# A second weight tile fetched from ScalarE's queue, and a branch that takes its row tiles in another order

## The chip, the cores and the metric

The kernel runs on one core of one Trainium2 chip. The metric is the device time of one execution in microseconds (us). The engines are named as the profile names them: PE is TensorE (PEld its weight loads), DVE is VectorE, ACT is ScalarE, POOL is GpSimd, and SP is SyncE, which here only issues DMAs. A DMA is issued by an engine's instruction stream (SPq, ACTq and POOLq in the profile) and carried out by 16 DMA engines that all queues of the core share.

## The reference

One layer of a decoder with two token mixers side by side, 256 tokens, 2048 channels, all in float32:

```python
h = rmsnorm(x, pre_norm_g[l])
proj = h @ w_in[l]                      # 2048 x 18448
(a_q, a_k, a_v, a_g, a_lr, b_q, b_k, b_v, b_g, m_a, m_b) = jnp.split(proj, offsets, axis=-1)
gk = log_sigmoid(a_lr @ gla_gk_w2[l] + gla_gk_b[l]) / 16
o_a = rmsnorm(gla_chunked(a_q, a_k, a_v, gk), gla_norm_g[l]) * silu(a_g)
y_a = o_a @ w_branch_a[l]               # 2048 x 2048
o_b = rmsnorm(diff_attention(b_q, b_k, b_v, lam), diff_norm_g[l]) * (1 - lam_init) * silu(b_g)
y_b = o_b @ w_branch_b[l]
merged = sigmoid(m_a) * y_a + sigmoid(m_b) * y_b
x = x + rmsnorm(merged @ w_out[l], post_norm_g[l])
```

Each `@` sums over 2048 rows of a weight matrix. The order in which these rows are summed is free.

## The kernel before, in words

**Tiles.** The 2048 rows of every matrix product are cut into 16 row tiles of 128 (`KT`; a row tile's index is `kt`). The host lays the weights out in pieces, in the order in which the kernel takes them. A piece is fetched by DMA into a tile `raw`, and is then split in two: ACT copies it rounded into `hi` (L345), DVE subtracts to get the rest `lo` (L346). PE multiplies `hi` with both halves of the other operand and `lo` with its first half (L519). The other operand is split in the same way: x into the tiles `xs`, two row tiles in each.

**The start.** The first weight chunk, `v0`, comes in 16 units of 416 KB (128 x 832), one row tile each. For a unit PE does four matmuls with `hi` into banks `mm`, four with `hi` into `bg`, and two and two with `lo`. Unit 0's weight `raw_first` is fetched as two halves of 208 KB. x comes transposed in groups of 1, 1, 2, 4, 4 and 4 row tiles (`load_x`), of 128 KB for each row tile, into `xraw`. x is multiplied by the gains `pre_norm_g` on its way to `xs` (`prep_x`: L390 on ACT or, for row tile 1, L388 on DVE gives the first half, L391 on DVE the second); the gains are an input of 8 KB, `preg_s`, fetched on ACT's queue as its first instruction. All other loads at the start are issued by SP in the order in which the code is written: x row tile 0, the two halves of `raw_first`, unit 1's weight, x row tile 1, x row tiles 2 and 3, unit 2's weight, unit 3's weight, and so on.

**Order.** The compiler's scheduler sorts the instructions of each engine from the order of the code and from when it reckons that the operands are there; `tc.keep_in_program_order` pins an instruction to its place. Weights are fetched and split `AHEAD` = 4 steps before their use; `raw` has 6 buffers.

**The second branch's first operand.** The output of the first token mixer is split into `oah` and `oal` and stored to DRAM in four pairs of 512 KB tiles. Later `fetch_a` loads the pairs 0, 1, 2, 3 back with SP (L816), `oah` and then `oal` of each. The chunks `y00` to `y03` multiply them with `w_branch_a`, eight units of two row tiles to a chunk. Which pair row tile `kt` lies in is told by `a_ops`:

```python
h, j = kt // 4, kt % 4
i = 2 * (h // 2) + j // 2               # the pair
return oah[i][:, j % 2, h % 2, :], oal[i][:, j % 2, h % 2, :]
```

So the units of `y00` use the pairs 0, 1, 0, 1, 2, 3, 2, 3. Between two units of `y00` PE does six matmuls of another product, recorded at L720 (`set`).

Of the kernel before, what the change touches and what calls it, by code (L numbers as in the profile page):

```python
# [6 lines left out]
F32 = mybir.dt.float32  # L7
# [7 lines left out]
P = 128  # L15
D = 2048
S = 256
KT = D // P
# [3 lines left out]
VG = (416, 416, 416, 416, 400)  # L22
RANK = 16
AHEAD = 4
X_GROUPS = ((0, 1), (1, 1), (2, 2), (4, 4), (8, 4), (12, 4))
X_LOADS = ((), (4,), (8,), (12,), (), (), (), ())
ROWS = {"two": 2, "tok": 4, "chan": KT}
# [130 lines left out]
def order_of(n):  # L158
    return OUT_ORDER if n == OUT else ORDERS[n not in MOVED]


def chain_of(n, name):
    if n == OUT:
        return OUT_CHAINS.get(name)
    chain = PRODUCTS[name][1]
    return chain if chain is None else (chain + n) % 2
# [3 lines left out]
def hybrid_kernel(ctx: ExitStack, tc, xt, xn, preg, postg, w, w2, gkb, glag, lamv, diffg, ident_d, causal_d, lmask_d, out):  # L170
    nc = tc.nc
    pe, act, dve, pool, sp = nc.tensor, nc.scalar, nc.vector, nc.gpsimd, nc.sync

    const = ctx.enter_context(tc.tile_pool(name="const", bufs=1))
    wpool = ctx.enter_context(tc.tile_pool(name="wpool", bufs=3))
# [7 lines left out]
    def u(shape, name, dtype=F32):  # L183
        count[0] += 1
        return big.tile(shape, dtype, tag="u", name=f"{name}_{count[0]}")
# [17 lines left out]
    def f32(ap):  # L203
        return ap.bitcast(F32)
# [17 lines left out]
    def piece(key, q):  # L222
        size = sizes[key]
        at = begins[key] + q * size * P
        return w[at : at + P * size].rearrange("(p n) -> p n", p=P)
# [4 lines left out]
    def block(n, name, unit, add=True, which=None, queue=pool):  # L230

        chain, (kh, g) = chain_of(n, name), which or PRODUCTS[name][2]
        src = piece(SETS[n][g], 2 * kh + unit // 2)[:, 1024 * (unit % 2) : 1024 * (unit % 2) + 1024]
        dst = chains[chain][unit] if chain is not None else plain[n, name, unit]
        if add:
            return pool.dma_start(dst, src, accum_op=ALU.add)  # L236
        return queue.dma_start(dst, src)  # L237
# [40 lines left out]
    def emit_half():  # L278
        j = emitted[0]
        emitted[0] += 1  # L280
        key, unit = steps[j]
        if j in begin:
            start_sets()
        if j == begin_out:
            start_out()
        if j == begin_out + 8:
            for n in range(4):
                plain[OUT, "p2", n] = u([P, 1024], "plain")
                block(OUT, "p2", n, add=False)
        if isinstance(key, int):  # L290
            i = set_steps.index((key, unit))
            name, part = order_of(key)[unit // 4], unit % 4
            if key == 1 and part == 0 and unit < 24:
                ahead = PRODUCTS[order_of(key)[unit // 4 + 1]][0]
                if ahead in parts_far:
                    fetch_square(ahead)
            chain, (kh, g) = chain_of(key, name), PRODUCTS[name][2]
            if (key, name, part) in plain:
                raw = plain.pop((key, name, part))
            elif chain is None:  # L300
                raw = wpool.tile([P, 1024], F32, tag="raw", name=f"raw_s{key}_{unit}", bufs=6)
                at = 1024 * (part % 2)
                sp.dma_start(raw, piece(SETS[key][g], 2 * kh + part // 2)[:, at : at + 1024])
            else:
                raw = chains[chain][part]
            hi_t = wpool.tile([P, 1024], F32R, tag="hi", name=f"hi_{j}")
            lo_t = wpool.tile([P, 1024], F32R, tag="lo", name=f"lo_{j}")
            act.activation(hi_t, raw, AF.Copy)  # L308
            dve.tensor_tensor(out=lo_t, in0=raw, in1=f32(hi_t), op=ALU.subtract)  # L309
            refill(i, key, name, part, raw)  # L310
            ready[j] = ((key, unit), hi_t, lo_t)
            return
        size = sizes[key]
        h = unit % 2
        src = piece(key, unit // 2)
        n = size // 2
        early = key == "v0"
        if j == 2:
            load_x(2, 2)
        if j == 0:  # L320
            raw = raw_0
        else:
            raw = wpool.tile([P, 1024], F32, tag="raw", name=f"raw_{key}_{unit}", bufs=6)
            i = sp.dma_start(raw[:, :n], src[:, n * h : n * h + n])
        if early:
            if j:
                tc.keep_in_program_order(i)
            if j == 1:
                load_x(1, 1)
            for kt in X_LOADS[j // 2] if h else ():  # L330
                load_x(kt, 4)
        if early:
            prep_x(j)
            if 6 <= j < 14:
                square_x(j - 6)
        if key == "o3" and j + 1 < len(steps):
            hi_t, lo_t = u([P, 1024], "keep", F32R), u([P, 1024], "keep", F32R)
        else:
            hi_t = wpool.tile([P, 1024], F32R, tag="hi", name=f"hi_{j}")
            lo_t = wpool.tile([P, 1024], F32R, tag="lo", name=f"lo_{j}")  # L340
        fine = 2 if j == 0 else 1
        for i in range(fine):
            a, b = n * i // fine, n * (i + 1) // fine
            r = raw[:, a:b]
            act.activation(hi_t[:, a:b], r, AF.Copy)  # L345
            dve.tensor_tensor(out=lo_t[:, a:b], in0=r, in1=f32(hi_t[:, a:b]), op=ALU.subtract)  # L346
        ready[j] = (key, hi_t, lo_t)
# [5 lines left out]
    def take(key):  # L353
# [3 lines left out]
        used[0] += 1  # L357
        while emitted[0] < min(j + 1 + AHEAD, len(steps)):
            emit_half()
# [6 lines left out]
    preg_s = const.tile([P, KT], F32, name="preg_s")  # L366
# [3 lines left out]
    def load_x(kt, n):  # L370
        tc.keep_in_program_order(sp.dma_start(xraw[kt // 4][:, kt % 4 : kt % 4 + n, :].rearrange("p a t -> p (a t)"), xt[P * S * kt : P * S * (kt + n)].rearrange("(p n) -> p n", p=P)))
# [3 lines left out]
    for c in (slice(0, VG[0]), slice(VG[0], 2 * VG[0])):  # L375
        tc.keep_in_program_order(sp.dma_start(raw_0[:, c], piece("v0", 0)[:, c]))
    act.preload_act_table_set("natural_log_exp_and_others")

    def x_ops(kt):
        return xs[kt // 2][:, kt % 2, 0, :], xs[kt // 2][:, kt % 2, 1, :]  # L380

    def prep_x(kt):
        i, j = kt // 4, kt % 4
        src = xraw[i][:, j, :]
        g = preg_s[:, kt : kt + 1]
        hi, lo = x_ops(kt)
        if kt == 1:
            dve.tensor_scalar(out=hi, in0=src, scalar1=g, scalar2=None, op0=ALU.mult)  # L388
        else:
            act.activation(hi, src, AF.Copy, scale=g)  # L390
        dve.scalar_tensor_tensor(out=lo, in0=src, scalar=g, in1=f32(hi), op0=ALU.mult, op1=ALU.subtract)  # L391
# [3 lines left out]
    def square_x(i):  # L395
        src = xraw[i // 2][:, 2 * (i % 2) : 2 * (i % 2) + 2, :].rearrange("p a t -> p (a t)")
        t = t2([P, 512], "xsq") if i else ssum
        tc.keep_in_program_order(act.activation(t, src, AF.Square))
        if i:
            dve.tensor_tensor(out=ssum, in0=ssum, in1=t, op=ALU.add)  # L400
# [280 lines left out]
    def start_sets():  # L681
        n = started[0]
        started[0] += 1
        while "squares" not in done:
            with tc.issue_after(latest[0]):
                next(operands, None)
        for c in range(2):
            chains[c][:] = [u([P, 1024], f"chain{c}") for _ in range(4)]
        for unit in range(4):
            tc.keep_in_program_order(block(n, "p1", unit, add=False))  # L690

    def start_out():
        for c in range(2):
            chains[c][:] = [u([P, 1024], f"chain{c}") for _ in range(4)]
        for unit in range(4):
            block(OUT, "p1", unit, add=False)
        for unit in range(4):
            block(OUT, "q7", unit, add=False, which=(1, 1))
        for unit in range(4):
            block(OUT, "q7", unit)  # L700

    def fetch_square(name):
        parts[name] = tuple(u([P, 8, P], "square", F32R) for _ in range(2))
        for t, src in zip(parts[name], parts_far[name]):
            tc.keep_in_program_order(pool.dma_start(f32(t), src))
# [469 lines left out]


    def a_ops(kt):
        h, j = kt // 4, kt % 4
        i = 2 * (h // 2) + j // 2
        return oah[i][:, j % 2, h % 2, :], oal[i][:, j % 2, h % 2, :]  # L1180

# [48 lines left out]
    first, both, raw = {}, {}, {}  # L1230
# [287 lines left out]
```

## Time and profile before

| | |
|---|---|
| time, median of 3 runs | 1090.03 us (1089.81 to 1090.1) |
| the profiled execution | 1090.54 us, of which its span in the trace is 1088.7 us |
| PE busy | 1078.1 us, 99% of the span |
| DVE, ACT, POOL busy | 871.1, 707.5, 219.6 us (80%, 65%, 20%) |
| granted TensorE clock | 0.997 |
| HBM | 276.71 MB read, 24.12 MB written, 276 GB/s over the span |

In a row of the timeline stand the start in us from the span's start, the duration in us, the engine, the line, the operation and what it writes and reads; in brackets, how long the engine was idle before it and what ended that. Rows of DMA issues give the time that the issue took, not the transfer; the time from an issue to its landing is in the DMA view (last column). L numbers are lines of this kernel; in the changed kernel the same lines stand 3 to 8 lines further down.

### The profile page before, as it was taken

What the parts mean: (1) busy time and instruction counts of PE and PEld (TensorE: products, weight loads), DVE (VectorE), ACT (ScalarE), POOL (GpSimd) and SP (SyncE); (2) the same over time, 40 slices, a digit from 0 to 9 for tenths busy, and PEclk for the clock granted to TensorE, in tenths of its full rate; (3) what the DMA queues carried; (4) which work ended last, traced back from release to release, by engine and by line L of the source; (5) the groups of instructions that cost most, each with busy time, mean ns of one, the idle gap of its engine ahead of it and who ended that gap; (6) DMA issues with size and microseconds to landing.
All of it is one profiled execution on the core that took longest, in us unless ns stands there. A gap on an engine that the chain in (4) does not pass through costs nothing.

```text
span 1088.7 us, 15454 instructions
## 1 busy us (share of the span) xinstructions
PE 1078.1 (99%) x5434; PEld 920.2 (85%) x5434; DVE 871.1 (80%) x1220; ACT 707.5 (65%) x1020; POOL 219.6 (20%) x319
## 2 busy tenths in 40 slices
PE   9999999999999999999999999999999999999996
PEld 8999888888888888888888888888888888888885
DVE  7787668997877889897887788776688687687994
ACT  8777466655656676776766767665666665536871
POOL 0112101110331222123113122222211222301100
PEclk9999999999999999999999999999999999999998
DMA  8899988598999988579989998999977999987874
GB/s 319 272 303 331 302 281 221 171 365 327 242 291 340 341 252 209 202 210 270 283 265 238 309 262 225 277 326 363 326 203 263 335 345 354 359 320 230 216 189 152
DMA packets 86286, 301.84 MB, mean 277 GB/s; under 512 B 10369, under 2 KB 11649, under 8 KB 86209
## 3 DMA queue, kind: packets, MB, share of 16 engines
q0 software_dynamic: 38560, 139.48, 49.2%
q1 hardware_dynamic: 46928, 160.33, 40.5%
q10 hardware_dynamic: 720, 1.06, 0.3%
q8 instruction: 42, 0.69, 0.2%
q14 instruction: 36, 0.29, 0.1%
HBM read 276.71 MB, written 24.12 MB: 276 GB/s over the span
## 4 chain that ended last, share of the span: by engine, by line
PE 96%; DMA 2%; DVE 0%; ACT 0%; POOL 0%; issue 0%; SPq 0%; DVEq 0%; POOLq 0%; ACTq 0%
PE mm L519 31%; PE set L720 31%; PE mm L540 16%; PE mm L542 8%; PE mm L501 2%; DMA oal<-oal_far 2%; PE bg L519 2%; PE bg L1039 1%; PE bg L906 1%; PE bg L501 1%; PE bg L1070 0%; DMA raw_v<-in_w_dram 0%; PE bg L1258 0%; PE bg L988 0%; PE bg L1077 0%; PE bg L1078 0%
## 5 line engine op out<-in xcount | busy, mean ns | idle before, releaser
L309 DVE TENSOR_TENSOR lo<-chain,hi 128x1024 fp32r<-128x1024 f32 x212 | 257.3, 1222 | 72.0 <-ACT hi L308 71.0
L308 ACT ACTIVATE hi<-chain 128x1024 fp32r<-128x1024 f32 x212 | 223.1, 1058 | 132.7 <-PE mm L519 45.0
L540 PE MATMUL mm<-xs,hi 128*128 128x512 f32 x768 | 199.6, 392 | 0.0
L236 POOL DMA_DIRECT2D chain<-in_w_dram x120 | 104.4, 874 | 436.5 <-DVE lo L309 288.1
L540 PEld LDWEIGHTS mm<-xs,hi 128*128 128x128 f32 x768 | 142.7, 188 | 28.1 <-ACT hi L345 0.5
L720 PE MATMUL set<-hi,square 128*128 128x512 f32 x512 | 139.6, 394 | 0.0
L519 PE MATMUL mm<-hi,xs 128*128 128x512 f32 (+2 forms) x512 | 118.9, 372 | 0.8 <-ACT hi L345 0.8
L542 PEld LDWEIGHTS mm<-xs,lo 128*128 128x128 f32 x768 | 104.5, 190 | 8.0 <-DVE lo L346 0.5
L720 PEld LDWEIGHTS set<-hi,square 128*128 128x128 f32 x512 | 93.4, 188 | 18.4 <-ACT qk L1168 0.7
L542 PE MATMUL mm<-xs,lo 128*128 128x256 f32 x768 | 107.2, 282 | 0.0
L720 PE MATMUL set<-hi,xs 128*128 128x512 f32 x384 | 104.8, 394 | 0.0
L519 PEld LDWEIGHTS mm<-hi,xs 128*128 128x128 f32 x512 | 94.7, 188 | 11.5 <-ACT hi L345 1.1
L346 DVE TENSOR_TENSOR lo<-raw_y,hi 128x1024 fp32r<-128x1024 f32 x64 | 78.3, 1223 | 31.0 <-ACT hi L345 30.8
L345 ACT ACTIVATE hi<-raw_y 128x1024 fp32r<-128x1024 f32 x64 | 67.9, 1061 | 53.9 <-PE mm L519 34.2
L720 PEld LDWEIGHTS set<-hi,xs 128*128 128x128 f32 x384 | 70.2, 188 | 13.3 <-ACT hi L308 0.3
L720 PE MATMUL set<-lo,square 128*128 128x512 f32 x256 | 79.2, 390 | 0.0
L237 POOL DMA_DIRECT2D chain<-in_w_dram x72 | 39.6, 556 | 159.4 <-DVE lo L309 128.9
L519 PE MATMUL mm<-lo,xs 128*128 128x512 f32 (+2 forms) x256 | 64.7, 369 | 0.0
L720 PE MATMUL set<-lo,xs 128*128 128x512 f32 x192 | 59.5, 391 | 0.0
L720 PEld LDWEIGHTS set<-lo,square 128*128 128x128 f32 x256 | 47.9, 188 | 10.9 <-DVE lo L309 0.5
L346 DVE TENSOR_TENSOR lo<-raw_dk,hi 128x1024 fp32r<-128x1024 f32 x32 | 39.1, 1222 | 18.6 <-ACT hi L345 18.6
L519 PEld LDWEIGHTS mm<-lo,xs 128*128 128x128 f32 x256 | 47.7, 188 | 5.5 <-DVE lo L346 0.3
(308 smaller groups left out, 1945.4 us busy)
## 6 DMA issues: line engine op xcount, KB each, us to landing
chain<-in_w_dram POOLq DMA_DIRECT2D x192, 512.0 KB, 10.3
raw_y<-in_w_dram SPq DMA_DIRECT2D x64, 512.0 KB, 8.0
raw_dq<-in_w_dram SPq DMA_DIRECT2D x32, 512.0 KB, 7.7
raw_dk<-in_w_dram SPq DMA_DIRECT2D x32, 512.0 KB, 7.6
raw_v<-in_w_dram SPq DMA_DIRECT2D x31, 416.0 KB, 5.4
raw_s<-in_w_dram SPq DMA_DIRECT2D x24, 512.0 KB, 8.0
raw_ag<-in_w_dram SPq DMA_DIRECT2D x24, 512.0 KB, 6.6
raw_k<-in_w_dram SPq DMA_DIRECT2D x16, 512.0 KB, 7.2
```

Of the source, the lines that this page charges most:

```text
L236: return pool.dma_start(dst, src, accum_op=ALU.add)
L237: return queue.dma_start(dst, src)
L308: act.activation(hi_t, raw, AF.Copy)
L309: dve.tensor_tensor(out=lo_t, in0=raw, in1=f32(hi_t), op=ALU.subtract)
L345: act.activation(hi_t[:, a:b], r, AF.Copy)
L346: dve.tensor_tensor(out=lo_t[:, a:b], in0=r, in1=f32(hi_t[:, a:b]), op=ALU.subtract)
L501: i = pe.matmul(out, lhs, rhs, start=first and n == 0, stop=last and n == len(pairs) - 1)
L519: i = pe.matmul(banks[g][b][:, :n], a[part][:, P * b : P * b + P], w[:, c : c + n], start=first, stop=last)
L540: i = pe.matmul(o, hi[:, c], x_pair(kt), start=kt == 0, stop=kt == KT - 1)
L542: i = pe.matmul(o[:, :S], lo[:, c], x_ops(kt)[0], start=False, stop=False)
L720: i = pe.matmul(bank, a[part], wt[:, 512 * j : 512 * j + 512], start=go, stop=end, skip_group_check=not first)
L906: pe.matmul(o, xk[:, P * c : P * c + P], xq.rearrange("p (b c t) -> p b c t", b=2, c=4)[:, :, c, :], start=i == 0, stop=i == 1)
```

## The change

The diff, with what lies between its parts left out:

```diff
+A_ORDER = (0, 1, 4, 5, 2, 3, 6, 7, 8, 9, 12, 13, 10, 11, 14, 15)
...
         if j == 0:
             raw = raw_0
+        elif j == 1:
+            raw = raw_1
         else:
             raw = wpool.tile([P, 1024], F32, tag="raw", name=f"raw_{key}_{unit}", bufs=6)
             i = sp.dma_start(raw[:, :n], src[:, n * h : n * h + n])
         if early:
-            if j:
+            if j > 1:
                 tc.keep_in_program_order(i)
...
     act.preload_act_table_set("natural_log_exp_and_others")
+    raw_1 = wpool.tile([P, 1024], F32, tag="raw", name="raw_second", bufs=6)
+    dve.tensor_copy(raw_1[:, :KT], preg_s)
+    tc.keep_in_program_order(act.dma_start(raw_1[:, : 2 * VG[0]], piece("v0", 0)[:, 2 * VG[0] :]))
...
     def a_ops(kt):
-        h, j = kt // 4, kt % 4
+        h, j = A_ORDER[kt] // 4, A_ORDER[kt] % 4
...
+    mats["w_branch_a"] = mats["w_branch_a"].reshape(KT, P, D)[list(A_ORDER)].reshape(D, D)
```

Unit 1's weight is no longer issued by SP but by ACT, into the tile `raw_second`. DVE first copies the gains into a corner of that tile; the DMA overwrites the copy, and so it can't be issued before the copy is done, nor the copy before the gains have landed. In SP's queue everything behind moves up by one place. The row tiles of `w_branch_a` and of its operand are permuted alike, so that the units of `y00` to `y03` use the pairs 0, 0, 1, 1, 2, 2, 3, 3.

The scheduler answers with another order at the start. On ACT, before (the tiles `hi` are numbered, `xs_72` holds the row tiles 0 and 1, `xs_73` 2 and 3; the rows begin behind the gains' DMA):

```order
L390 ACTIVATE xs_72<-xraw_81,preg_s 128x256
L345 ACTIVATE hi_177<-raw_first 128x416 x2
L345 ACTIVATE hi_188<-raw_v_1_183 128x832
L390 ACTIVATE xs_73<-xraw_81,preg_s 128x256 x2
L345 ACTIVATE hi_197<-raw_v_2_193 128x832
```

and in the changed kernel:

```order
L396 ACTIVATE xs_72<-xraw_81,preg_s 128x256
L383 DMA raw_second<-in_w_dram 128x832
L348 ACTIVATE hi_180<-raw_first 128x416 x2
L396 ACTIVATE xs_73<-xraw_81,preg_s 128x256 x2
L348 ACTIVATE hi_189<-raw_second 128x832
```

The issue of the DMA has come in behind x's row tile 0, and the split of unit 1's weight now stands behind x's row tiles 2 and 3 instead of ahead of them.

On DVE at the start, before (L388 and the L391 behind it are x's row tile 1):

```order
L391 SCALAR_TENSOR_TENSOR xs_72<-xraw_81,preg_s,xs_72 128x256
L346 TENSOR_TENSOR lo_178<-raw_first,hi_177 128x416 x2
L388 TENSOR_SCALAR xs_72<-xraw_81,preg_s 128x256
L391 SCALAR_TENSOR_TENSOR xs_72<-xraw_81,preg_s,xs_72 128x256
L346 TENSOR_TENSOR lo_189<-raw_v_1_183,hi_188 128x832
L391 SCALAR_TENSOR_TENSOR xs_73<-xraw_81,preg_s,xs_73 128x256 x2
```

and in the changed kernel:

```order
L382 COPY raw_second<-preg_s 128x16
L397 SCALAR_TENSOR_TENSOR xs_72<-xraw_81,preg_s,xs_72 128x256
L394 TENSOR_SCALAR xs_72<-xraw_81,preg_s 128x256
L397 SCALAR_TENSOR_TENSOR xs_72<-xraw_81,preg_s,xs_72 128x256
L349 TENSOR_TENSOR lo_181<-raw_first,hi_180 128x416 x2
L397 SCALAR_TENSOR_TENSOR xs_73<-xraw_81,preg_s,xs_73 128x256 x2
L349 TENSOR_TENSOR lo_190<-raw_second,hi_189 128x832
```

The copy is new; x's row tile 1 has moved ahead of unit 0's two `lo`, and the row tiles 2 and 3 ahead of unit 1's.

On PE in `y00`, one matmul of each of the first seven units, before (`oah_7032`, `_7139`, `_7260` and `_7270` are the pairs 0 to 3):

```order
L519 MATMUL mm_7274<-hi_7177,oah_7032 128x512
...
L519 MATMUL mm_7274<-hi_7229,oah_7139 128x512
...
L519 MATMUL mm_7274<-hi_7289,oah_7032 128x512
...
L519 MATMUL mm_7274<-hi_7331,oah_7139 128x512
...
L519 MATMUL mm_7274<-hi_7361,oah_7260 128x512
...
L519 MATMUL mm_7274<-hi_7390,oah_7270 128x512
...
L519 MATMUL mm_7274<-hi_7419,oah_7260 128x512
```

and in the changed kernel (`oah_7033`, `_7140`, `_7261` and `_7271` are the pairs 0 to 3):

```order
L525 MATMUL mm_7275<-hi_7178,oah_7033 128x512
...
L525 MATMUL mm_7275<-hi_7230,oah_7033 128x512
...
L525 MATMUL mm_7275<-hi_7290,oah_7140 128x512
...
L525 MATMUL mm_7275<-hi_7332,oah_7140 128x512
...
L525 MATMUL mm_7275<-hi_7362,oah_7261 128x512
...
L525 MATMUL mm_7275<-hi_7391,oah_7261 128x512
...
L525 MATMUL mm_7275<-hi_7420,oah_7271 128x512
```

Pair 3 is first used in the seventh unit instead of the sixth. Apart from these places, the order on the five engines differs only in a few neighbours that have changed places.

## The prediction

> **What bounds the kernel now.** I read the page's busy times and its chain first, then who made PE wait, then the two places where it did.
>
> ```profile
> PE 1078.1 (99%) x5434; PEld 920.2 (85%) x5434; DVE 871.1 (80%) x1220; ACT 707.5 (65%) x1020; POOL 219.6 (20%) x319
> ...
> PE 96%; DMA 2%; DVE 0%; ACT 0%; POOL 0%; issue 0%; SPq 0%; DVEq 0%; POOLq 0%; ACTq 0%
> ```
>
> PE is busy for 1078.1 of 1088.7 us, and 96% of the chain is PE. What isn't PE's own work can be gained only where PE waits. The waits of PE in the whole span (who waited for whom; total us, times, longest) are three:
>
> ```profile
> PE bg L434 <- DVE ones L431: 1.1, 1, 1.1
> PE mm L519 <- ACT hi L345: 0.8, 1, 0.8
> PE mm L519 <- DMA oal<-oal_far: 0.5, 1, 0.5
> ```
>
> The first lies ahead of the warm-up matmuls and isn't touched. The second is at unit 1's start, the third in `y00`: the change aims at these two. Since PE has no other wait, whatever it loses or gains at them goes through to the end.
>
> The start, in the timeline:
>
> ```profile
> 0.74 0.41 ACTq L373 DMA_DIRECT2D preg_s<-in_preg_dram  x1
> ...
> 2.12 0.43 SPq L324 DMA_DIRECT2D raw_v<-in_w_dram  x1
> ...
> 2.60 0.91 SPq L371 DMA_DIRECT2D xraw<-in_xt_dram  x2
> ...
> 3.06 0.51 ACT L390 ACTIVATE xs<-xraw,preg_s 128x256 fp32r<-128x256 f32 x1 [0.28 <-DMA preg_s<-in_preg_dram]
> 3.54 0.91 SPq L324 DMA_DIRECT2D raw_v<-in_w_dram  x2
> 3.60 0.48 DVE L391 SCALAR_TENSOR_TENSOR xs<-xraw,preg_s,xs 128x256 fp32r<-128x256 f32 x1 [2.59 <-ACT xs L390]
> 3.67 0.55 ACT L345 ACTIVATE hi<-raw_first 128x416 fp32r<-128x416 f32 x1
> 4.25 0.59 DVE L346 TENSOR_TENSOR lo<-raw_first,hi 128x416 fp32r<-128x416 f32 x1 [0.17 <-ACT hi L345]
> ...
> 4.40 1.01 PE L519 MATMUL mm<-hi,xs 128*128 128x416 f32 x4
> ...
> 4.80 0.55 ACT L345 ACTIVATE hi<-raw_first 128x416 fp32r<-128x416 f32 x1 [0.57 <-DMA raw_first<-in_w_dram]
> ...
> 5.40 1.02 PE L519 MATMUL bg<-hi,xs 128*128 128x416 f32 x4
> ...
> 6.64 0.54 PE L519 MATMUL bg<-lo,xs 128*128 128x416 f32 x2
> ...
> 7.02 0.90 ACT L345 ACTIVATE hi<-raw_v 128x832 fp32r<-128x832 f32 x1 [1.67 <-DMA raw_v<-in_w_dram]
> 7.36 0.35 DVE L388 TENSOR_SCALAR xs<-xraw,preg_s 128x256 fp32r<-128x256 f32 x1 [1.38 <-DMA xraw<-in_xt_dram]
> ...
> 7.75 0.48 DVE L391 SCALAR_TENSOR_TENSOR xs<-xraw,preg_s,xs 128x256 fp32r<-128x256 f32 x1
> ...
> 7.97 1.02 PE L519 MATMUL mm<-hi,xs 128*128 128x416 f32 x4 [0.79 <-ACT hi L345]
> 8.01 0.91 ACT L390 ACTIVATE xs<-xraw,preg_s 128x256 fp32r<-128x256 f32 x2
> 8.15 1.02 DVE L346 TENSOR_TENSOR lo<-raw_v,hi 128x832 fp32r<-128x832 f32 x1
> ```
>
> Unit 0 ends at 7.18 (6.64 + 0.54) and unit 1 begins at 7.97, 0.05 behind the end of its `hi`, which began as soon as its weight had landed. In the chain the piece is
>
> ```profile
> 2.12 4.88 DMA raw_v<-in_w_dram
> ```
>
> so the weight landed at 7.00. When the other early loads landed I work out from their issues above and their times to landing (DMA view, one narrow window for each):
>
> ```profile
> raw_first<-in_w_dram SPq DMA_DIRECT2D x1, 208.0 KB, 3.1
> ...
> xraw<-in_xt_dram SPq DMA_DIRECT2D x1, 128.0 KB, 4.7
> ...
> xraw<-in_xt_dram SPq DMA_DIRECT2D x1, 256.0 KB, 4.9
> ...
> raw_v<-in_w_dram SPq DMA_DIRECT2D x1, 416.0 KB, 5.5
> ...
> raw_v<-in_w_dram SPq DMA_DIRECT2D x1, 416.0 KB, 6.1
> ```
>
> `raw_first`'s second half lands at about 4.8 (the `hi` that waits for it starts at 4.80), x row tile 1 at 2.60 + 4.7 = 7.3, row tiles 2 and 3 at some 3.06 + 4.9 = 8.0, unit 2's weight at 3.54 + 5.5 = 9.0, unit 3's at some 4.0 + 6.1 = 10.1. Each lands behind the one issued before it.
>
> **Part A: unit 1's weight on ACT's queue.** It removes one of SP's issues (0.43 us), so x's row tiles 1, 2 and 3 and the weights behind them are issued that much earlier; that alone is worth nothing to PE, which waits for none of them.
>
> The new copy on DVE (128x16; nearest row L388 with 256 columns, 0.35 us, an upper end) can start when the gains are there, by 3.06, and is over before DVE's next step at 3.60: its cover is DVE's idle time of 2.59 us. ACT issues `raw_second` behind its first `xs`, at about 3.5, instead of SP at 2.12. The issue (0.41, the gains' row) holds up the ACT work queued behind it, `hi` of `raw_first`: 3.67 becomes some 4.0, and PE's first matmul 4.7 instead of 4.40. That is hidden: the `hi` of the second half can't start before 4.80 anyway, so `bg` starts at about 5.45 instead of 5.40.
>
> What costs is which bytes have to land before unit 1. Before, unit 1's weight was behind 8 + 128 + 416 KB; with its own 416 KB, 968 KB. Now x's 128 and 256 KB are ahead of it on SP's queue and in flight at the same time, and ACT does `xs` of the row tiles 2 and 3 ahead of unit 1's `hi`: 1352 KB have to land first. In the trace of before, the same 1352 KB were in at about 8.0. If `raw_second` is the last of them, its `hi` ends at 8.0 + 0.90 and unit 1 starts at 8.95, 1.0 later than 7.97. If x's row tiles 2 and 3 are the last, their `xs` (0.91) come in between: 9.85. If unit 2's weight, issued by SP at about the same time as `raw_second` by ACT, takes its share too, `raw_second` may land as late as 9.0: 9.95, or +2.0. I take a landing at 8.3, nearest to the row of the same bytes, with a little for unit 2's share: unit 1 starts at 9.25, **+1.3**.
>
> The other end: DVE now does x's row tile 1 ahead of unit 0's `lo`. That tile can land no earlier than 0.3 behind `raw_first` (as it did behind unit 1's weight, 7.3 against 7.0), at 5.1; L388 and L391 take until the next step 8.15 - 7.36 = 0.79, two `lo` 1.18, so unit 0's last matmuls start at about 7.1 and end at 7.6. And `raw_second` can't well be in before 3.5 + 3.1 = 6.6, the time of a transfer of half its size: unit 1 at 7.55. So A gains 0.4 at most. Even a `raw_second` that is early would gain little, since unit 0 has become later. Range of A: -0.4 to +2.0.
>
> Behind unit 1 nothing more is lost: unit 2's `hi` is ready 0.9 behind unit 1's, while PE has 2.3 us of work in each unit.
>
> **Part B: the order of the row tiles in `y00`.** It adds and removes no instruction; the host permutes the weights. The chain's piece, the landing of pair 2's `oal` in the DMA view, and PE's rows at the start of the units four to six (counted from 0) and of the unit behind:
>
> ```profile
> 733.88 18.50 DMA oal<-oal_far
> ...
> oal<-oal_far SPq DMA_DIRECT2D x1, 512.0 KB, 16.0
> ...
> 747.45 0.39 PE L519 MATMUL mm<-hi,oah 128*128 128x512 f32 x1
> ...
> 751.53 0.39 PE L519 MATMUL mm<-hi,oah 128*128 128x512 f32 x1
> 752.42 0.50 PE L519 MATMUL mm<-hi,oal 128*128 128x512 f32 x1 [0.51 <-DMA oal<-oal_far]
> ...
> 756.41 0.39 PE L519 MATMUL mm<-hi,oah 128*128 128x512 f32 x1
> ```
>
> A unit with its companion takes 751.53 - 747.45 = 4.08 us; the one with the wait 756.41 - 751.53 = 4.88. The wait with its slower restart costs **0.8**, more than the 0.5 that the list of waits gives. In the new order pair 3 is first wanted one unit later, at 751.53 + 4.08 = 755.61, 3.2 behind its landing at 752.38: the wait is gone whole. Pair 2 is wanted at 747.45 as before and landed at about 728 + 16.0 = 744; pair 1 is wanted later than before. What is late next would be the weights of `y00`; but the `hi` of that stage waits for PE to free its buffers, and for a weight's DMA only once in the kernel, in the last chunk:
>
> ```profile
> ACT hi L345 <- PE mm L519: 58.9, 44, 2.6
> ...
> ACT hi L345 <- DMA raw_o<-in_w_dram: 4.0, 1, 4.0
> ```
>
> So B is worth -0.8, between 0 (if the transfer lands over 3.2 later) and -0.8.
>
> **The sum.** +1.3 - 0.8 = +0.5. The profiled execution took 1090.54 (span 1088.7 and 1.84 around it), so it would take 1091.0; it was 0.51 above the median of the runs shown, against which I forecast **1090.5**. About 0.2%, 2.2 us, is what a measurement of this kernel can tell from no change. Both waits together are below that, so I expect no change that can be told.
>
> **The rivals.**
> *1. Two queues feed the DMA engines better than one, and A gains.* For it: the DMA engines have a hole just where unit 1's weight should flow. Their traffic in windows of 1 us (busy time of each engine, clock, DMA share, GB/s):
>
> ```profile
> 4.00:5.00 1.00, 1.00 (x7) 1.00 (x7) 0.67 (x2) 0.42 (x2) 0.00 (x0) 1.00 0.67 193
> ...
> 7.00:8.00 1.00, 0.21 (x2) 0.03 (x1) 0.61 (x2) 0.90 (x1) 0.00 (x0) 1.00 1.01 350
> ```
>
> If a second queue fills the hole, (350 - 193) KB, or 0.45 us, are won, and if `raw_second` is served first it lands between 6.6 and 7.4: A between -0.4 and +0.4, the time 1088.8 to 1089.6, say 1089.3. Against it: the share is 1.01 by 7 us, so afterwards the two queues share what one had, and `raw_second` is issued 1.4 us later than unit 1's weight was. [...]
>
> *2. Slower: `raw_second` lands behind the weights of the units 2 and 3.* SP issues these at 3.54 and 4.0, when ACT gets to its own issue, and they landed by 9.0 and 10.1. Landing at 10.1, unit 1 starts at 11.05, +3.1, and with B the time is 1092.3. It counts as slower from a landing at 10.0 on (7.97 + 0.8 + 2.2 - 0.95). Against it: `raw_second` doesn't have to stand in SP's queue behind them.
>
> *3. B gains nothing*, since pair 3 lands still later or another tile takes its place as the one waited for: with A as above 1091.3. Against it: 3.2 us to spare, and no change in SP's order there.
>
> **How the numbers follow.** The main case, A between +0.8 and +2.0 with B whole: 0.62 (1090.0 to 1091.2). Rival 1: 0.22. Rival 2: 0.08. Rival 3: 0.05. The rest 0.03 is for waits that I don't see. The range 1088.9 to 1091.6 takes in the main case, rival 3 and nearly all of rival 1, and leaves out rival 2 and the rest. Slower by over 0.2% (above 1092.2): most of rival 2 and a little of the rest, 0.08. Faster by over 0.2% (below 1087.9): both waits gone are worth some 1.6 even where all is gained, so 0.02. Within: 0.90.
>
> **What the changed kernel's profile would show.** B right: no wait of PE for `oal`, and units of 4.08 us throughout `y00`. A right: unit 1's first matmul at about 9.25 (8.9 to 10.0), its `hi` behind two `xs`, ahead of it a wait of ACT for `raw_second` or for x, a longer wait of PE than 0.79, and unit 0's last `lo` matmuls later than 6.64. A wrong: unit 1 at or ahead of 7.97 (rival 1), or behind 10.95 (rival 2). A new wait of PE anywhere else would make the forecast wrong.

## The result, and the profile after

The changed kernel takes 1095.84 us (median of 6 runs, 1091.64 to 1098.92) against 1090.28 (6 runs, 1089.81 to 1090.57) for the kernel before: a ratio of 1.005, interval 1.003 to 1.0069. It is slower by 5.6 us, outside the range that was forecast. The profiled execution took 1096.0, its span is 1094.2, 5.5 more than before, at a mean granted clock of 0.994 instead of 0.997.

The page's busy times and its chain, after:

```profile
PE 1080.9 (99%) x5434; PEld 923.3 (84%) x5434; DVE 872.1 (80%) x1221; ACT 707.7 (65%) x1020; POOL 219.1 (20%) x319
...
PE 96%; issue 1%; DMA 1%; DVE 1%; ACT 0%; POOL 0%; DVEq 0%; POOLq 0%; ACTq 0%
```

PE is still the bound, with 2.8 us more busy time for the same 5434 matmuls. Its waits in the whole span:

```profile
PE mm L525 <- ACT hi L348: 3.8, 1, 3.8
PE bg L440 <- DVE ones L437: 1.1, 1, 1.1
```

The wait for `oal` is gone. The one at unit 1, 0.8 before, is now 3.8. The timeline there, with PE's rows up to the start of unit 3:

```profile
3.10 0.17 DVE L382 COPY raw_second<-preg_s 128x16 f32<-128x16 f32 x1 [2.10 <-DMA preg_s<-in_preg_dram]
...
3.30 0.34 ACTq L383 DMA_DIRECT2D raw_second<-in_w_dram  x1
...
4.49 1.73 PE L525 MATMUL mm<-hi,xs 128*128 128x416 f32 x4
...
7.41 0.91 ACT L396 ACTIVATE xs<-xraw,preg_s 128x256 fp32r<-128x256 f32 x2 [2.24 <-DMA xraw<-in_xt_dram]
...
7.60 0.64 PE L525 MATMUL bg<-lo,xs 128*128 128x416 f32 x2
...
11.13 0.90 ACT L348 ACTIVATE hi<-raw_second 128x832 fp32r<-128x832 f32 x1 [2.80 <-DMA raw_second<-in_w_dram]
...
12.08 1.76 PE L525 MATMUL mm<-hi,xs 128*128 128x416 f32 x4 [3.83 <-ACT hi L348]
...
16.40 1.12 PE L525 MATMUL mm<-hi,xs 128*128 128x416 f32 x4
...
18.86 0.92 PE L525 MATMUL mm<-hi,xs 128*128 128x416 f32 x4
```

Unit 0 is over at 8.24 (7.60 + 0.64); `raw_second` lands at 11.1, and unit 1 starts at 12.08 instead of 7.97. What else stands ahead of it was there long before: x's row tiles 2 and 3, whose `xs` ACT does ahead of unit 1's `hi`, at 7.41. Then unit 1 itself takes 16.40 - 12.08 = 4.32 us instead of the 2.38 before (10.35 - 7.97), with the same matmuls: four of them 1.76 instead of 1.02. The end of unit 1 before is read from the first row of unit 2 there:

```profile
10.35 0.92 PE L519 MATMUL mm<-hi,xs 128*128 128x416 f32 x4
```

The DMA view (last column: us from issue to landing), one narrow window each for the weight of unit 2 (issued by SP at 3.06), of unit 3 (SP, some 3.5) and of unit 1 (ACT, 3.30):

```profile
raw_v<-in_w_dram SPq DMA_DIRECT2D x1, 416.0 KB, 7.1
...
raw_v<-in_w_dram SPq DMA_DIRECT2D x1, 416.0 KB, 8.0
...
raw_second<-in_w_dram ACTq DMA_DIRECT2D x1, 416.0 KB, 7.8
```

They land at 10.2, 11.5 and 11.1: the weight that is needed first comes after unit 2's. How the two hardware queues shared the DMA engines (packets, MB, share of the time of 16 engines; q10 carries only what ACT issues) in the windows 7 to 8 and 9 to 10:

```profile
q10 hardware_dynamic: 69, 0.20, 48.9%
q1 hardware_dynamic: 60, 0.17, 42.5%
...
q1 hardware_dynamic: 108, 0.38, 98.7%
q10 hardware_dynamic: 8, 0.03, 6.5%
```

From 7 to 8 us ACT's queue has about half of the engines' time (48.9%). From 9 to 10 its share is 6.5%, as much as one engine in 16 all the time, or two half of it. The single packets say the same. From its issue to its landing, 144 packets run on ACT's queue: the weight's 128 of 3328 bytes, and 16 small ones of under 512 bytes, read here as the reports that a part is in. Of these, 14 had come by 8.25, the last two come at 10.5 and 10.8, and `hi` begins at 11.13, 0.3 behind the last. Between 8.25 and 8.6 ACT's queue moves no packet at all, and then 18: two reports and 16 of the weight's data packets. The trace doesn't name a packet's engine. As an estimate, if each of 16 engines has the same part, 128 / 16 = 8 packets and a report, the 126 packets up to 8.25 are 14 whole parts and the 18 behind it two. By it 14 engines were done in time, and two began with this weight only at 8.6, while SP's packets ran on.

That the two queues moved 69 and 60 packets side by side between 7 and 8 doesn't show in what order an engine takes packets of both. Why the last two reports came 2.3 and 2.6 us behind the other 14 (the last of these at 8.2) the trace doesn't show either.

The second loss is in the clock. Windows of 2 us (busy time of PE, PEld, DVE, ACT and POOL, granted clock, DMA share, GB/s):

```profile
8.00:10.00 2.00, 0.25 (x2) 0.00 (x0) 0.84 (x2) 0.32 (x1) 0.00 (x0) 1.00 1.02 372
10.00:12.00 2.00, 0.00 (x0) 0.00 (x0) 0.00 (x0) 0.87 (x2) 0.00 (x0) 0.50 1.02 395
12.00:14.00 2.00, 1.92 (x6) 1.86 (x7) 1.94 (x3) 2.00 (x5) 0.00 (x0) 0.50 1.02 417
14.00:16.00 2.00, 2.00 (x7) 1.94 (x6) 2.00 (x5) 2.00 (x4) 0.00 (x0) 0.50 1.02 379
16.00:18.00 2.00, 2.00 (x10) 1.94 (x10) 1.44 (x3) 0.55 (x2) 0.00 (x0) 0.80 0.97 333
```

While PE waited, its clock was halved, at 10.0 and so 1.8 us into the wait, and it stayed so for 2 + 2 + 2 + 0.8 = 6.8 us (0.80 over 2 us is 0.8 us at half), 4.7 of them after unit 1 had started. Both losses together stand in one row: the small matmul behind chunk `v0` that sums the squares (first and last start), before

```profile
L453 PE MATMUL bg<-ones,ssum x8: 166/251/251, 35.3 to 36.0; 128*128 128x2 f32 x8
```

and after

```profile
L459 PE MATMUL bg<-ones,ssum x8: 166/251/251, 41.5 to 42.2; 128*128 128x2 f32 x8
```

It has moved by 6.2: 4.1 by the later start of unit 1, and 2.1 more behind it, which the filler below shows to be the clock. The rest of the kernel gives back 0.7, since the whole span is only 5.5 longer. `y00` has become shorter by about as much. PE's units four to six there start at (timeline, after):

```profile
754.06 0.39 PE L525 MATMUL mm<-hi,oah 128*128 128x512 f32 x1
...
758.14 0.39 PE L525 MATMUL mm<-hi,oah 128*128 128x512 f32 x1
...
762.22 0.39 PE L525 MATMUL mm<-hi,oah 128*128 128x512 f32 x1
```

Unit five takes 4.08 like unit four, its 4.88 is gone: unit four starts 6.6 later than before, unit six 5.8. The smaller shifts between the sum's matmul and `y00` (6.2 to 6.6) and behind it (5.8 to 5.5) aren't explained. Together it is 4.1 + 2.1 - 0.7 = 5.5, the difference of the spans.

### The profile page after: what moved, and what is told of

Same layout as the page of the kernel before. It is cut to its first block, busy times and chain, and to the rows that moved or that the text cites. A ratio compares the mean times of both kernels' runs of the same rounds, so it can differ in the third digit from the quotient of the medians.

```text
span 1094.2 us, 15454 instructions
## 1 busy us (share of the span) xinstructions
PE 1080.9 (99%) x5434; PEld 923.3 (84%) x5434; DVE 872.1 (80%) x1221; ACT 707.7 (65%) x1020; POOL 219.1 (20%) x319
## 3 DMA queue, kind: packets, MB, share of 16 engines
q0 software_dynamic: 38560, 139.48, 48.9%
## 4 chain that ended last, share of the span: by engine, by line
PE 96%; issue 1%; DMA 1%; DVE 1%; ACT 0%; POOL 0%; DVEq 0%; POOLq 0%; ACTq 0%
PE mm L525 31%; PE set L726 31%; PE mm L546 16%; PE mm L548 8%; PE mm L507 2%; PE bg L525 2%; PE bg L1045 1%; PE bg L912 1%; PE bg L507 1%; DMA raw_second<-in_w_dram 1%; PE bg L1076 0%; PE bg L1264 0%; PE bg L1138 0%; PE bg L994 0%; PE bg L1084 0%
```

## The experiments

Two numbers serve throughout: where unit 1 starts, and where that small matmul (`ssum`, below "the sum's matmul") starts. Without a loss between them they lie 27.3 us apart, as in the kernel before (35.3 - 7.97). The medians are set against those of the kernel before on the same chip.

| kernel | unit 1 | sum's matmul | apart | median less that of before | ratio, interval |
|---|---|---|---|---|---|
| before, first profile | 7.97 | 35.3 | 27.3 | | |
| before, once more | 8.16 | 35.4 | 27.2 | | |
| row order alone | 8.46 | 35.8 | 27.3 | -0.3 | 0.9993, 0.9985 to 1.0002 |
| row order and halves | 8.06 | 35.5 | 27.4 | 0.0 | 1.0002, 0.9993 to 1.0011 |
| no hold, longer warm-up | 8.36 | 35.6 | 27.2 | +0.1 | 0.9999, 0.9990 to 1.0008 |
| one queue | 9.53 | 36.8 | 27.3 | +0.8 | 1.0009, 0.9999 to 1.0019 |
| no hold | 9.55 | 36.7 | 27.2 | +1.2 | 1.0013, 1.0004 to 1.0022 |
| SP's rest held | 8.55 | 37.5 | 29.0 | +2.0 | 1.0019, 1.0009 to 1.0029 |
| filler | 11.43 | 38.7 | 27.3 | +2.6 | 1.0023, 1.0014 to 1.0032 |
| second queue alone | 11.85 | 40.6 | 28.8 | +4.2 | 1.0033, 1.0024 to 1.0043 |
| after, once more | 11.53 | 41.6 | 30.1 | +4.8 | 1.0043, 1.0030 to 1.0057 |
| after | 12.08 | 41.5 | 29.4 | +5.6 | 1.0050, 1.0030 to 1.0069 |

### Each part alone

The kernel before with the new row order and nothing else:

```diff
+A_ORDER = (0, 1, 4, 5, 2, 3, 6, 7, 8, 9, 12, 13, 10, 11, 14, 15)
...
-        h, j = kt // 4, kt % 4
+        h, j = A_ORDER[kt] // 4, A_ORDER[kt] % 4
...
+    mats["w_branch_a"] = mats["w_branch_a"].reshape(KT, P, D)[list(A_ORDER)].reshape(D, D)
```

> Part B alone: only the row tiles of the second branch are permuted, the start is as before. Theory 1 (the parts add up; B removes a wait worth 0.8 us): 0.8 us faster than before, no wait of PE for oal, one wait of 0.8 us left at unit 1, time about 1089.4. Theory 2 (part of the changed kernel's loss comes from the new order in the branch): slower than before, or equal.

Measured: 1090.04 (12 runs) against 1090.36 (35 runs). PE doesn't wait for `oal`, but the gain of 0.3 is less than the 0.8 expected and can't be told from none. By the interval the new order costs at most 0.2 us, and what it saves is at most 0.15%, 1.6 us.

The changed kernel with the old row order:

```diff
-A_ORDER = (0, 1, 4, 5, 2, 3, 6, 7, 8, 9, 12, 13, 10, 11, 14, 15)
+A_ORDER = tuple(range(16))
```

> Part A alone: unit 1's weight on ACT's queue with the hold, the row tiles in the old order. Theory 1: the whole loss is here, 4.1 us of waiting and about 2.1 us at half clock: some 6.3 us slower than before (1096.5), unit 1 at about 12, with a spread over the runs like the changed kernel's, and the wait for oal back. Theory 2: clearly less than 6 us.

Measured: 1094.54 against 1090.36. Of PE's rows at unit 1, and the windows around it:

```profile
11.85 1.75 PE L525 MATMUL mm<-hi,xs 128*128 128x416 f32 x4 [3.74 <-ACT hi L348]
```

```profile
10.00:12.00 2.00, 0.15 (x1) 0.15 (x1) 0.17 (x1) 1.10 (x2) 0.00 (x0) 0.90 1.01 402
12.00:14.00 2.00, 2.00 (x6) 1.92 (x7) 2.00 (x3) 2.00 (x4) 0.00 (x0) 0.50 1.04 418
14.00:16.00 2.00, 2.00 (x9) 1.94 (x9) 1.95 (x5) 2.00 (x5) 0.00 (x0) 0.75 1.05 367
```

The loss comes with the second queue: the same wait, and half the clock for 0.4 + 2 + 1 = 3.4 us. Here that is one half of the 6.8 of the changed kernel, and the distance to the sum's matmul is 28.8 instead of 29.4. The median is 4.2 above before where 6.3 was expected; that it is less than the changed kernel's 4.8 and 5.6 can't be told, since the intervals overlap. The old row order is in this kernel, and yet its list of waits shows none for `oal`, which was expected back. That was the first sign that the wait which part B removes isn't in every execution.

The changed kernel again, unchanged:

> The changed kernel, unchanged, a second profile beside the kernel before on the same chip. Theory 1 (the weight is late in every execution, the clock falls in most): the weight lands at 10 to 11.5 again with its last packets on one or two DMA engines, unit 1 starts at 11 to 12.5, the clock falls to half for 0, 3.4 or 6.8 us, and the time is 3 to 6 us above before. Rival (the profile of the changed kernel showed a rare disturbance): unit 1 at 9 to 9.5 as forecast, and the time within 1.5 us of before.

```profile
10.58 0.90 ACT L348 ACTIVATE hi<-raw_second 128x832 fp32r<-128x832 f32 x1 [1.49 <-DMA raw_second<-in_w_dram]
...
11.53 1.76 PE L525 MATMUL mm<-hi,xs 128*128 128x416 f32 x4 [3.33 <-ACT hi L348]
```

Measured: 1094.63 against 1089.81. `raw_second` lands at 10.6, against 11.1 and 10.9 in the two traces above: late every time, by a little more or less. Here 13 of its 144 packets come behind 9.0, the last of them behind 10.

### Is it the queue, or what shares the engines with it?

The changed kernel, with unit 2's weight made to wait for `raw_second`, by a copy of one column into its buffer; until `raw_second` has landed, SP's queue then carries only `raw_first` and x's first row tiles:

```diff
+            if early and j == 2:
+                pool.tensor_copy(raw[:, :1], raw_1[:, :1])
             i = sp.dma_start(raw[:, :n], src[:, n * h : n * h + n])
```

> The changed kernel with SP held back: a copy of one column from unit 1's weight into unit 2's buffer makes SP issue unit 2's weight, and all behind it, only when unit 1's weight has landed. Beside it only x's row tiles 1 to 3 are then in flight. Theory 1 (taking turns with SP's weights makes it late): it lands by 7.5, on the last DMA engines too, and unit 1 starts by 8.5; unit 2, whose weight is issued only then, waits instead, to about 12. Rival (ACT's queue is slow by itself on some DMA engines): it lands at 10 to 11 all the same.

The timeline and, from the DMA view, the landing:

```profile
7.59 0.90 ACT L350 ACTIVATE hi<-raw_second 128x832 fp32r<-128x832 f32 x1
...
8.55 1.02 PE L527 MATMUL mm<-hi,xs 128*128 128x416 f32 x4 [0.34 <-ACT hi L350]
...
12.47 1.03 PE L527 MATMUL mm<-hi,xs 128*128 128x416 f32 x4 [1.40 <-ACT hi L350]
```

```profile
raw_second<-in_w_dram ACTq DMA_DIRECT2D x1, 416.0 KB, 4.3
```

Issued at 3.30 as in the changed kernel, it lands at 7.6 instead of 11.1, and unit 1 starts at 8.55. So ACT's queue isn't slow by itself, and the hold alone doesn't make the landing late; what makes it late is the weights that SP's queue carries beside it. What is held pays for it: unit 2 (12.47) waits 1.4, and the median is 1091.83 against 1089.88.

The kernel before, with x's row tiles 1, 2 and 3 put ahead of unit 1's weight on SP's queue, so that the bytes ahead of that weight are those of part A, but all in one queue:

```diff
-        if j == 2:
+        if j == 1:
+            load_x(1, 1)
             load_x(2, 2)
...
-            if j == 1:
-                load_x(1, 1)
```

> The kernel before with x's row tiles 1, 2 and 3 issued by SP ahead of unit 1's weight, all on one queue: the order of the bytes of the changed kernel without ACT's queue. Theory 1 (the second queue is what makes the weight late): the weight lands at about 8.0, where the same 1352 KB were in before, unit 1 starts at about 9.0, no fall of the clock, 1.0 us slower than before (1091.2). Rival (having x's bytes and x's work on ACT and DVE ahead of unit 1 is what costs): unit 1 starts at 11 to 12 as in the changed kernel, some 6 us slower than before.

```profile
raw_v<-in_w_dram SPq DMA_DIRECT2D x1, 416.0 KB, 5.5
```

```profile
9.53 1.03 PE L518 MATMUL mm<-hi,xs 128*128 128x416 f32 x4 [1.33 <-ACT hi L344]
```

Measured: 1091.12 against 1090.36. Issued at 3.07, unit 1's weight lands at 8.6, later than the 8.0 expected, and in this trace the clock stays up (1.00, and 1.03 for unit 1's four matmuls). The same bytes in one queue cost unit 1 some 1.6 us, in two queues 4.1. Three of the ten runs took 1092.6 to 1093.6 at a mean clock of 0.996, the others had 0.997 or 0.998 (one of them took 1093.7 all the same): the clock may have fallen in the three, but none of them was traced.

### What the clock costs

The changed kernel, with 14 matmuls of a constant tile (recorded as 28) on PE between unit 0 and unit 1, to fill the wait:

```diff
+FILL = 14
...
+            if groups == 2 and q == 0:
+                filler = ps("bg")
+                for _ in range(FILL):
+                    tc.keep_in_program_order(pe.matmul(filler[:, :P], ones, ones, start=True, stop=True))
```

> The changed kernel with 14 extra matmuls of ones (128x128) on PE between unit 0 and unit 1, where PE otherwise waits; their result is not used. Theory 1 (the long wait makes the granted clock fall to half, and that costs 2.1 us beside the wait): the granted clock stays at 1.00 up to 20 us, unit 1 takes 2.3 to 2.4 us instead of 4.3, the time is some 2 us below the changed kernel's, about 1093.7, and its spread is smaller. Rival (the clock at the start is a matter of the warm-up and not of the wait): unit 1 is as slow as without the filler, and the time is that of the changed kernel or higher by what of the filler sticks out.

The timeline, and the window behind unit 1's start:

```profile
7.62 3.29 PE L531 MATMUL bg<-ones 128*128 128x128 f32 x28
...
11.43 1.02 PE L526 MATMUL mm<-hi,xs 128*128 128x416 f32 x4 [0.52 <-ACT hi L349]
```

```profile
12.00:14.00 2.00, 2.00 (x13) 1.97 (x12) 2.00 (x3) 1.75 (x4) 0.00 (x0) 1.00 1.03 417
```

Unit 1 is still late, but its four matmuls take 1.02, the clock is 1.00, and the distance to the sum's matmul is the 27.3 of the kernel before. In this trace it isn't the weight that sets unit 1's start: `raw_second` lands at 10.2, x's row tiles 2 and 3 at 9.7 instead of 7.4, and their `xs` on ACT, ahead of unit 1's `hi`, end only at 10.6. Measured: 1092.99 against 1090.36, +2.6, where the changed kernel has +4.8 and +5.6. That is 2.2 to 3.0 less by the medians, and it takes in a start of unit 1 that is 0.1 to 0.65 earlier here; by the distances (29.4 and 30.1 against 27.3) 2.1 to 2.8 us of the loss are the clock, and the rest is the wait.

The traces without a filler bear this out. From unit 1's start on, the clock is at half for 3.1 us with the second queue alone, for 4.7 in the changed kernel and for 6.1 in its second profile (up to 17.6), and the distance has grown by 1.5, 2.1 and 2.8: each time a little under half of that stretch.

### Are the two waits that the change aimed at there at all?

The kernel before, profiled once more:

> The kernel before, unchanged, a second profile. If the wait for pair 3's oal belongs to the order of the row tiles, it is there again with 0.5 us. If it is a matter of when that transfer happens to land (two kernels with the old order had no such wait, with 17.3 us to landing against 18.5), it may be gone, and the landing is then below about 18 us.

Its timeline, its only wait of PE, and how long `oal`'s loads and stores took (DMA view of that tile):

```profile
4.63 1.75 PE L519 MATMUL mm<-hi,xs 128*128 128x416 f32 x4
...
8.16 0.92 PE L519 MATMUL mm<-hi,xs 128*128 128x416 f32 x4
```

```profile
PE bg L434 <- DVE ones L431: 1.1, 1, 1.1
```

```profile
DMA to landing us min/median/max: 6.3/12.1/17.3
```

Neither is there. Unit 0 ran at half speed at its start (1.75 for four matmuls, 1.01 in the first profile), so PE was busy until unit 1's weight had come; unit 1 starts only 0.2 later, at 8.16. And pair 3's `oal`, issued at 733.9 as before, landed 17.3 later instead of 18.5: at 751.2, just ahead of the 751.5 at which it is wanted. This execution took 1089.39, less than the 1090.54 of the first profile. So neither wait is there in every execution of this kernel. That at unit 1 comes in other sizes too: with the same start, the kernel with the row order alone waits 0.4 there.

### Two ways to have the wait at unit 1 shorter

The changed kernel without DVE's copy, so that nothing holds back ACT's DMA:

```diff
-    dve.tensor_copy(raw_1[:, :KT], preg_s)
```

> The changed kernel without the copy that holds the DMA back: ACT issues unit 1's weight behind its table load, at about 2.5 instead of 3.3. Theory 1 (the weight is late because its packets take turns with those of SP's queue, on the slowest DMA engines with three to four packets a window): less of SP's work is in flight beside it, it lands 1 to 2 us earlier, unit 1 at 9.5 to 11, still later than before (7.97), and raw_first lands a little later; some 1 to 4 us slower than before. Theory 3 (the late issue is the cause): unit 1 at 8 or earlier and no loss against before.

```profile
1.21 0.42 ACTq L382 DMA_DIRECT2D raw_second<-in_w_dram  x1
...
5.53 1.76 PE L524 MATMUL mm<-hi,xs 128*128 128x416 f32 x4 [0.69 <-ACT hi L348]
...
9.55 0.92 PE L524 MATMUL mm<-hi,xs 128*128 128x416 f32 x4
```

Measured: 1091.11 against 1089.88. The issue comes at 1.21 instead of the 2.5 expected, beside that of unit 0's weight (SP, from 1.18 on), and `raw_second` lands at some 5.1 (3.9 behind it). Now it is `raw_first` that is late, with 3.8 us to landing (median of its halves) instead of the 2.8 before: unit 0 starts at 5.53, with a wait of 0.69 ahead of it, and its four matmuls take 1.76 instead of 1.01. That unit 1 starts at 9.55, within the 9.5 to 11 expected, is luck: the weight was expected to land only 1 to 2 us earlier, and lands 6 earlier. The time has gone to unit 0, whose weight is now in flight together with unit 1's.

The same with two more of the matmuls ahead of unit 0 (`WARM` 10 instead of 8, recorded as 20 and 16):

> The changed kernel without the hold, and with 10 warm-up matmuls instead of 8. Without the hold, unit 1's weight landed at 5.0 and raw_first as a whole at 4.9, but PE stood still for 0.7 us ahead of unit 0 and then did unit 0 at half speed until about 9.4. Theory (the idle time ahead of unit 0 is what keeps the clock down, and the two queues themselves cost nothing at this place): with the gap filled, PE is at full speed by 7, unit 0 ends at 8 or earlier, unit 1 follows without a wait, and the time is that of before or up to 0.5 us below. Rival (the late raw_first is what costs, whatever the clock): unit 1 at 9 or later and 1 us slower than before, as without the extra matmuls.

```profile
6.00 1.01 PE L524 MATMUL mm<-hi,xs 128*128 128x416 f32 x4 [0.99 <-ACT hi L348]
...
8.36 0.92 PE L524 MATMUL mm<-hi,xs 128*128 128x416 f32 x4
```

Measured: 1089.92 against 1089.81. Unit 0 is later still but at full speed (1.01), and unit 1 follows it without a wait, at 8.36. The loss is gone, and nothing is gained. That the longer warm-up made the difference isn't shown: the intervals of the two kernels overlap a little, and in this trace PE seems to have been at full speed before the extra matmuls ran. The warm-up matmuls, with the longer warm-up and without:

```profile
1.06 3.95 PE L439 MATMUL bg<-ones 128*128 128x128 f32 x20 [1.06 <-DVE ones L436]
```

```profile
1.06 3.78 PE L439 MATMUL bg<-ones 128*128 128x128 f32 x16 [1.06 <-DVE ones L436]
```

At the pace of the second row, 0.24 each, 20 would take 4.7. In the filler's trace 28 of the same size took 3.29, 0.12 each. An estimate with 0.24 for each up to a change and 0.12 behind it puts the change at about 4.2, when some 13 were done; the 16 of before last longer than that.

The kernel before with the new row order, and unit 1's weight fetched and split in two halves on SP's queue:

```diff
-            i = sp.dma_start(raw[:, :n], src[:, n * h : n * h + n])
+            halves = 2 if key == "v0" and j == 1 else 1
+            for c in range(halves):
+                a, b = n * c // halves, n * (c + 1) // halves
+                i = sp.dma_start(raw[:, a:b], src[:, n * h + a : n * h + b])
...
-        fine = 2 if j == 0 else 1
+        fine = 2 if j < 2 else 1
```

> The kernel before with the new order of the row tiles, and with unit 1's weight left on SP's queue but fetched and split as two halves, like unit 0's. Theory: the first half lands about 1 us earlier than the whole, so PE's wait at unit 1 shrinks from 0.8 to 0.2 or less; with the wait for oal gone, 0.6 to 1.4 us faster than before (about 1089.3). Rival: the halves only move the wait to the second half or to x's row tile 1, and the time is that of the new order alone.

```profile
8.06 0.62 PE L523 MATMUL mm<-hi,xs 128*128 128x416 f32 x2
```

Measured: 1089.90 against 1089.88. A miss: unit 1 starts at 8.06 without a wait in PE's list, and no time is gained. A likely reason is that the first profile's 0.8 isn't there to be won in most executions. No version that was run beats the kernel before by what can be told.

## Why the prediction was wrong

**The landing of `raw_second`, the step that failed.** Part A took 8.3, with 9.0 as its later end; it was 11.1, 10.9 and 10.6 in the three traces of this queue without a filler, and 10.2 with it. The step counted the bytes that have to land first and read the time off the one queue of before. In one queue that nearly holds: 8.6, when the order alone is changed. In two queues the bytes didn't come in such an order. The argument against rival 2, that `raw_second` needn't stand in SP's queue behind the weights of the units 2 and 3, was true and no help: issued 0.24 behind unit 2's weight and ahead of unit 3's, it shared the engines' time with SP's queue (48.9% against 42.5% from 7 to 8) and landed between those weights (10.2 and 11.5), 0.3 behind its last report. For most of it the 8.3 was nearly right: 14 of the 16 reports had come by 8.25, and with the 0.3 from the last report to the landing that is an estimated 8.5. The last two reports, at 10.5 and 10.8, make the 11.1. Rival 2 came nearest (a landing at 10.1 and unit 1 at 11.05), with a chance of 0.08 that was far too small, and without the clock: its 1092.3 is still 3.5 short. What is shown: with SP's weights held, the weight lands at 7.6. What stays open: why, beside them, its last packets came so much later than the others.

**"Behind unit 1 nothing more is lost", the second step.** It left out the clock. Waits of 0.8 to 1.4 had no such price in the traces, those of 3.3 to 3.8 had: half the clock for 3.4 or 6.8 us, 1.5 to 2.8 us more until the sum's matmul (28.8 to 30.1 against 27.3). That it isn't always the same length fits the spread of the six runs: the one at 1091.64 had a mean clock of 0.998, the others 0.994 to 0.996.

**Part B.** Right in the profile: no wait for `oal`, units of 4.08 throughout, some 0.8 less in that trace. As a gain over the kernel's runs it was too large: the wait was in one of the two profiles of before, and in neither of the two others with the old row order (old order with the second queue, and one queue). Alone it is worth 0.3 by the medians, between -0.2 and 1.6 by the interval. One reading behind it was wrong, and nothing hung on it: `hi` waits for a weight's DMA not only in the last chunk, but at the start too (1.67 for unit 1's weight).

**The wait of 0.8 at unit 1** was taken for a property of the kernel. It came out differently in three traces with the same start: 0.79 where unit 0's first four matmuls took 1.01 and unit 1's `hi` began at 7.02, none with 1.75 and 7.00, and 0.40 with 1.76 and 7.51 (row order alone). It was used only as the base from which unit 1's start is counted, so it did little harm: 8.16 instead of 7.97.

**The small steps held.** The copy on DVE and the issue on ACT cost nothing that PE sees. ACT's issue came at 3.30 instead of 3.5, unit 0's last matmuls at 7.60, later than 6.64 as forecast, and later than the forecast 7.1, in a trace whose unit 0 began at half speed. Rival 1 is excluded by the landing. What the prediction set against it, that the two queues share what one had, agrees with the window from 7 to 8 (48.9% and 42.5% of the 16 engines' time, 100.9% for the one queue of before); that the bytes therefore come at nearly the same times as in one queue, which the +1.3 took for granted, does not agree with the landings (11.1, 10.9 and 10.6).

The sum, by the same terms: the start of unit 1 +4.1 (forecast +1.3), the clock +2.1 (forecast nothing), part B and the rest of that trace -0.7 (forecast -0.8).

## What to carry to other kernels

A load on a second queue need not come ahead of what the first queue has in flight: here it shared the engines' time with it, and two of its 16 reports came 2.3 and 2.6 us behind the others. The same bytes ahead of unit 1 let its weight land at 8.6 in one queue and at 10.6 to 11.1 in two. So for an urgent load a place ahead of the others in one queue is the first thing to try; holding the others back brought it in earlier too (7.6), but the kernel was 2.0 us slower all the same. A long wait of PE can have a second price, the clock behind it: here 1.5 to 2.8 us beside waits of 3.3 to 3.8, and none beside waits up to 1.4; what lies between wasn't measured. And a wait of less than 1 us in a single profile should be looked for in a second profile before a change is built on it.

## What was not expected of the hardware

- Half the clock lasted 3.4 us with the second queue alone and 6.8, twice that, in both profiles of the changed kernel, behind waits of 3.3 to 3.8 us. It began when PE had been idle for 1.8 and 2.6 us in the profiles of the changed kernel, and for 3.5 us with the second queue alone. What sets its start and its length no run here shows.
- The clock column reads 1.00 from the start, while the same four matmuls of unit 0 take 1.01 us in one execution and 1.73 to 1.76 in another. At the start the column doesn't tell the pace of the matmuls, their durations do.
- ACT issued its DMA at 3.30, in the middle of its own activation (3.10 to 3.61): an issue behind an operation in the order didn't wait for its end here.
